# Slots from 256 on: from each expert's step to one place at the layer's end

## The chip, the cores and the metric

The kernel runs on one core of a Trainium2 chip. The metric is the device time of one execution in microseconds (us). Three runs of the kernel before gave 1459.17, 1465.08 and 1466.83; their median, 1465.08, is the time to which the prediction refers. One more execution was profiled and took 1460.41 us.

A core has five engines, each with an instruction stream of its own: PE (matrix products), ACT (ScalarE), DVE (VectorE), POOL (GpSimd) and SP (SyncE). In this kernel SP issues nearly all plain DMAs, and POOL issues the gathers and scatters through index lists (software DMA). The engines meet at semaphores.

## The reference

A decoder trunk of two layers over 512 tokens of width 1024, in float32. Each layer is a mixer (layer 0: dilated attention beside an mLSTM; layer 1: sparse attention) and a mixture of experts, each followed by a layer norm with a scaled residual. The change touches the experts alone:

```python
def hier_moe(x, wr_g, br_g, wr_e, br_e, w_gate, w_up, w_down):
    ...
    _, g_idx = lax.top_k(g_logits, 1)                 # one of 4 groups
    ...
    top_v, top_i = lax.top_k(e_logits, MOE_TOP_K)     # 2 of its 4 experts
    e_w = jax.nn.softmax(top_v, axis=-1) * g_w[:, None]
    ...
    h = jax.nn.silu(xc @ wg) * (xc @ wu)              # 16 experts, hidden 512
    h = h * gate of the expert                        # zero where not chosen
    return h @ wd
```

So each token is worked on by 2 of 16 experts. There are 512 x 2 = 1024 pairs of a token and an expert in a layer, 64 for an expert on average, and no bound on how many fall to one but the 512 tokens.

## The kernel before

**Slots and rounds.** A token row of 1024 is kept as two half rows of 512, so a tile of 128 partitions holds 64 tokens. The pairs of an expert are numbered as slots. A round is 64 slots. `route` (in `Moe`) counts the slots of each expert and leaves words with one bit per expert: `flags[0]` says more than 128 slots, `many[.., 1]` more than 64, `many[.., 2]` more than 192, `flags[3]` more than 256.

**The step.** `step(e)` (L1334) is laid out once per expert. On PE: the transposition of expert e's hidden values (`turn_hidden`), its second product for round 0 (`down`, L1190, 16 matmuls), the first product of the next expert, n = e + 1, for round 0 (`up`, L1162, 32 matmuls), then `beyond(e)`, then for each of n and e an If on more than 64 slots: a second round, or one matmul with zeros (`none`, L1168). ACT copies the result of round 0 to y0 (L1375), DVE that of round 1 to y1 (L1373). ACT and DVE together make the gated activation of n in between (`gated`, L1173 and L1174). POOL adds y0 and y1 into the layer's sum in DRAM (hacc) by scatter DMAs (`scatter`, L1122), and fetches the tokens of expert e + 4 (`fetch_rounds`, L1116). Since hacc is read and written by each scatter, y0 of a step waits until y1 of the step before has landed; y0 and y1 of one step hold other tokens and need not wait for each other. y0 and y1 have one buffer each, so ACT's next copy to y0 waits until y0's scatter has landed.

**Beyond 128 slots.** `beyond(e)` (L1193) is one If on `flags[0]` (L1223), the body of which does two rounds on the tile `more`: products, gated activation, two copies (L1218 on ACT, L1216 on DVE) and two scatters. The tokens have been fetched there by `fetch_beyond(e)`, an If of its own on POOL (the If itself is laid out at L1135, as all that go through `if_more`). Inside the body, a second If on `flags[3]` (L1226) does slots 256 to 511 in two more passes of two rounds, each with a gather of its own. All of this uses the weights of expert e while they are still in their buffers; `reload` then gives the buffers to later weights.

**Order.** `InOrder` keeps the order in which the program lays out instructions, on each of PE, ACT, DVE and POOL, and each of these passes each If whose body holds work for it. An engine that skips a body takes its way around, and a wait there holds all behind it. Weights come as 48 chunks of 2 MB a layer in a ring of nine, loaded by SP (L73 and, in four pieces, L77). SP issues in order.

**The end of a layer.** After the last step `run` (L1252) takes a tile for the norm's factors and loads them (`second_gb`, L1623, into `gb`), loads the sum back from hacc (`load_back`, L1437) and does the residual and the norm (`tail`): PE adds the last expert's result (`back`, L1462), DVE adds the two (`add`, L1469), then come the norm's statistics and products (L142 to L178). In layer 0 the last step also holds work on the next mixer's weights (`lows`, L101).

Of the kernel before, what the change touches and what calls it, by code (L numbers as in the profile page):

```python
# [8 lines left out]
F32 = mybir.dt.float32  # L9
# [6 lines left out]
ORDERED = (mybir.EngineType.PE, mybir.EngineType.Activation, mybir.EngineType.DVE)  # L16
# [3 lines left out]
S, D, P = 512, 1024, 128  # L20
NB = S // P
KT = D // P
E, H = 16, 512
# [191 lines left out]
def bank(k, name):  # L215
    return k.ps.tile([P, 512], F32, name=name, bufs={"acc": 2, "s": 2, "pt": 2, "x": 1, "o": 1}[name])
# [51 lines left out]
def run(steps):  # L268
    for f in steps:
        f()  # L270
# [223 lines left out]
def mixer_ab(k, a, moe, prefetch):  # L494
# [99 lines left out]
    bv = slot("c", (P, NB, 4, 129))  # L594
    nc.gpsimd.memset(bv[:, :, :, 128:129], 1.0)
    run(tokens_blocks(k, ch[3], XH, XL, lambda tb, ps: nc.scalar.copy(
        bv[:, tb, :, 0:128], ps.rearrange("p (h e) -> p h e", h=4))))
    loadnext(6)
# [12 lines left out]
    def ev_o(tb, ps):  # L611
        nc.scalar.activation(og[:, tb], ps, AF.Tanh, scale=0.5)
        nc.vector.scalar_tensor_tensor(og[:, tb], og[:, tb], 1.0, hgb, op0=OP.add, op1=OP.mult)

    run(tokens_blocks(k, ch[4], XH, XL, ev_o))
    loadnext(7)

# [332 lines left out]
class Moe:  # L950
# [234 lines left out]
    def down(self, py, h, r, chunk):  # L1185

        for q in range(4):
            c, b = divmod(q, 2)
            for w in range(2):
                self.k.nc.tensor.matmul(py[w * 64:w * 64 + 64], h[:, r, b, c * 64:c * 64 + 64],  # L1190
                                        chunk[q][:, w * 512:w * 512 + 512], start=q == 0, stop=q == 3)

    def beyond(self, e):  # L1193

        k, nc = self.k, self.k.nc
        w = [k.stream.raw[c] for c in k.ch_moe[self.layer][3 * e:3 * e + 3]]
        x = self.more
        s = x[:, 0].rearrange("p (r a) -> p r a", r=2)
        idx, wt = self.got[e]

        def rounds():
            t = self.xt.tile([P, 2, 4, P], F32, name="xm", bufs=1)
            self.turn(x, t)
            ps = [bank(k, "s") for _ in range(2)]
            self.up(ps[0], t, 0, w)
            self.if_more(ORDERED[0], 2, e, lambda: self.up(ps[1], t, 1, w), lambda: self.none(ps[1]))
            for r in range(2):
                self.gated(s[:, r], ps[r], wt[:, 2 + r, 1:2])
            h = t[:, 0].rearrange("p (r a) b -> p r a b", r=2)
            self.turn_hidden(s, h)  # L1210
            py = [bank(k, "s") for _ in range(2)]
            self.down(py[0], h, 0, w[2])
            self.if_more(ORDERED[0], 2, e, lambda: self.down(py[1], h, 1, w[2]), lambda: self.none(py[1]))
            for r in range(2):
                if r:
                    nc.vector.tensor_copy(x[:, r], py[r])  # L1216
                else:
                    nc.scalar.copy(x[:, r], py[r])  # L1218
            for r in range(2):
                self.scatter(x[:, r], idx[:, 2 + r:3 + r])  # L1220

        over = nc.snap(self.flags[0] & (1 << e))
        with k.tc.If(over > 0, label=f"over{self.layer}_{e}"):  # L1223
            rounds()
            many = nc.snap(self.flags[3] & (1 << e))
            with k.tc.If(many > 0):  # L1226
                for j in range(2, 4):
                    self.one_hot(e, self.oho, j * P)
                    pp = bank(k, "pt")[:, 0:12]
                    self.collect(e, self.oho, pp, 6)  # L1230
                    self.slots(e, 2, pp, 6)
                    for r in range(2):
                        self.fetch(x[:, r], idx[:, 2 + r:3 + r])
                    rounds()

    def load(self, m, queue=None):

# [14 lines left out]
    def run(self, following, finish):  # L1252


        k, nc, st = self.k, self.k.nc, self.k.stream
        pe, act, dve, pool = ORDERED + (mybir.EngineType.Pool,)
        self.rows = [k.moe.tile([P, 2, 512], F32, name=f"rows{i}", bufs=1) for i in range(4)]
        self.more = self.rows[3]
        self.ox = k.moe.tile([P, 2, P], F32, name="hs", bufs=2)
        self.oho = k.early.tile([P, NB, 2 * P], BF16, name="oho", bufs=1)  # L1260
        self.zeros = k.small.tile([P, 512], BF16, name="zeros")
        self.iota = k.small.tile([P, 2 * P], BF16, name="iota")
        self.xt = k.early
        self.got = {}
        self.oh, self.x, self.s = {}, {}, {}

        self.load(RING - 1)
        with k.order:
            nc.gpsimd.memset(self.zeros, 0.0)
            nc.vector.tensor_copy(self.iota.rearrange("p (r i s) -> p r i s", r=2, i=2),  # L1270
                                  k.iota.rearrange("p (r s) -> p r s", r=2)[:, :, None].to_broadcast([P, 2, 2, 64]))
            later, weights = self.route()
            for e in range(2):
                self.got[e] = self.place()
                self.hot(e, False)
                pp = bank(k, "ox"[e])[:, 0:2]
                self.collect(e, self.oh[e], pp, 1)
                self.slots(e, 0, pp, 1)
                self.fetch_rounds(e)
            nc.gpsimd.memset(self.oho, 0.0)  # L1280
            self.load(RING - 2, nc.gpsimd)
            ex = later()
            self.turned(0)
            weights(ex)
            for e in range(2):
                self.beyond_hot(e)
                self.find(e)
        self.order = InOrder(k, ORDERED + (pool,))
        with self.order:
            for e in range(-1, E):  # L1290
                self.step(e, following)
        gb, emit = finish()
        self.load_back(2, NB, after=k.gb_load)
        with self.order:
            self.tail(self.t, self.accs, gb, emit)
# [502 lines left out]
```

## Time and profile before

| | |
|---|---|
| runs, median (lowest, highest) | 1465.08 us (1459.17, 1466.83) |
| profiled execution | 1460.41 us, of which the span of instructions is 1458.5 us |
| busy: PE, DVE, ACT, POOL | 1268.8, 560.1, 410.1, 288.2 us |
| read from and written to DRAM | 287.29 MB and 35.69 MB |
| weights and other plain loads (queue q1) | 257.97 MB |
| software DMA (queue q0) | 39.42 MB |

The experts of layer 0 take the span from about 340 to 700 us, those of layer 1 from about 1060 to 1430 us. A busy engine is not an engine at its peak. The rows further down give a start in us from the span's start, a length in us, the engine, the line of the kernel, the operation with its tiles, how many instructions were merged into the row (x16), and in brackets how long the engine stood idle before it and what it waited for. "<-issue" means that nothing in the profile shows a reason. A "q" behind an engine's name is its sequencer, which does branches and waits.

### The profile page before, as it was taken

The page shows a single profiled execution, that of the slowest core. Times are in us where ns is not written, and L with a number is a line of the kernel's source. Part 1 is how long each engine was busy: PE and PEld are TensorE (multiplying, and loading weights), DVE is VectorE, ACT ScalarE, POOL GpSimd, SP SyncE. Part 2 cuts the span into 40 slices and gives each one's busy share as a digit, 9 for nine tenths or more (in the row PEclk, how much of TensorE's full clock was granted, in tenths as well). Part 3 has the DMA queues.
Part 4 walks back from the last instruction along what each step waited for, and adds up shares of the span by engine and source line. Part 5 has one row for each costly group of instructions (what it writes and reads, how often), then busy time and mean ns, then how long its engine had stood idle before and what let it go on. Part 6 is the DMA issues. An engine that isn't in the chain of part 4 may idle for free. (4 is left out here: it accounts for less than half of the span.)

```text
span 1458.5 us, 18462 instructions
## 1 busy us (share of the span) xinstructions
PE 1268.8 (87%) x6379; PEld 732.6 (50%) x6404; DVE 560.1 (38%) x1452; ACT 410.1 (28%) x852; POOL 288.2 (20%) x319
## 2 busy tenths in 40 slices
PE   7999999986889988898599999999779875877985
PEld 6777864573333333333277877777633322333332
DVE  4845644474211101211466546877631111221114
ACT  4333434441111000111235445655410010111112
POOL 2200000033222111322320000000422113222222
PEclk9999999986999999999899999999779998999998
DMA  8721250192797427899644530303725447999953
GB/s 296 247 94 58 93 210 22 68 365 81 306 351 289 185 61 278 281 390 337 240 163 151 224 123 15 146 22 143 298 99 191 178 141 251 376 395 384 370 151 145
DMA packets 64136, 299.80 MB, mean 206 GB/s; under 512 B 15426, under 2 KB 15586, under 8 KB 36560
## 3 DMA queue, kind: packets, MB, share of 16 engines
q1 hardware_dynamic: 42624, 257.97, 45.8%
q0 software_dynamic: 21328, 39.42, 9.8%
q8 instruction: 111, 1.82, 0.5%
q14 instruction: 73, 0.60, 0.1%
HBM read 287.29 MB, written 35.69 MB: 221 GB/s over the span
## 5 line engine op out<-in xcount | busy, mean ns | idle before, releaser
L1162 PE MATMUL acc<-raw,xt 128*64 128x512 f32 x1376 | 307.4, 600 | 7.0 <-PEq L1223 4.3
L1174 DVE SCALAR_TENSOR_TENSOR hs<-hs,wsl,acc 128x256 f32<-128x256 f32 x64 | 30.6, 480 | 471.2 <-ACT hs L1173 236.1
L1162 PEld LDWEIGHTS acc<-raw,xt 128*64 128x64 f32 x1376 | 102.7, 139 | 205.4 <-issue 185.7
L1122 POOL DMA_INDIRECT hacc<-y,idx x60 | 95.7, 1596 | 316.7 <-issue 138.6
L1190 PE MATMUL s<-raw,hm 128*64 128x512 f32 x464 | 119.1, 660 | 21.7 <-ACT hm L1183 13.1
L101 DVE TENSOR_TENSOR sl<-raw,sh 128x1024 fp32r<-128x1024 f32 x80 | 96.3, 1224 | 51.0 <-ACT sh L93 50.0
L1375 ACT COPY y<-s 128x512 f32<-128x512 f32 x30 | 17.6, 586 | 301.9 <-DMA hacc<-y,idx 278.0
L1116 POOL DMA_INDIRECT rows<-hmid,idx x72 | 75.7, 1052 | 102.2 <-issue 88.8
L93 ACT CAST sh<-raw 128x1024 fp32r<-128x1024 f32 x80 | 81.8, 1048 | 32.0 <-PE acc L119 10.7
L1190 PEld LDWEIGHTS s<-raw,hm 128*64 128x64 f32 x464 | 35.6, 151 | 86.0 <-issue 59.6
L1173 ACT ACTIVATE hs<-acc 128x256 f32<-128x256 f32 x64 | 24.6, 385 | 178.2 <-PE acc L1162 160.6
L1190 PE MATMUL s<-sh,hm 128*64 128x512 f32 x224 | 51.1, 598 | 8.3 <-ACT hm L1183 4.2
L1168 PE MATMUL s<-zeros 128*128 128x512 bf16 x23 | 10.1, 438 | 54.3 <-DVEq L1223 33.8
L1151 PE MATMUL pt<-ident,rows 128*128 128x128 f32 x288 | 45.8, 309 | 12.2 <-issue 6.4
L396 ACT ACTIVATE p<-p,smx 128x512 f32<-128x512 f32 (+1 forms) x96 | 54.0, 563 | 6.0 <-DVE smx L394 5.4
L394 DVE CUSTOM_DVE_ANT_0 p<-s,bt 128x384 f32<-128x384 f32 (+3 forms) x69 | 34.6, 503 | 49.5 <-PE s L877 34.5
L1151 PEld LDWEIGHTS pt<-ident,rows 128*128 128x128 f32 x288 | 38.1, 158 | 27.9 <-issue 25.0
L1162 PE MATMUL s<-raw,xm 128*64 128x512 f32 x160 | 42.7, 655 | 10.4 <-ACT xm L1155 9.6
L287 PE MATMUL acc<-sh,h 128*128 128x512 f32 x112 | 46.7, 417 | 0.2
L1168 PEld LDWEIGHTS <-zeros 128*128 128x128 bf16 x48 | 4.6, 96 | 83.5 <-issue 78.3
L477 POOL DMA_DIRECT2D bt<-rows x16 | 8.8, 552 | 190.2 <-DVE smx L394 188.3
L118 PE MATMUL acc<-h,sh 128*128 128x512 f32 x112 | 45.2, 403 | 0.0
(440 smaller groups left out, 2375.0 us busy)
## 6 DMA issues: line engine op xcount, KB each, us to landing
raw<-moe SPq DMA_DIRECT2D x168, 1024.0 KB
sh<-moe SPq DMA_DIRECT2D x40, 512.0 KB
raw<-cw SPq DMA_DIRECT2D x18, 1024.0 KB
raw<-abw SPq DMA_DIRECT2D x12, 1024.0 KB
rows<-row POOLq DMA_DIRECT2D x8, 640.0 KB
bt<-rows POOLq DMA_DIRECT2D x16, 256.0 KB
raw<-abo SPq DMA_DIRECT2D x4, 1024.0 KB
hmid<-s SPq DMA_DIRECT2D x8, 512.0 KB
```

Source lines behind the costliest of these rows:

```text
L93: k.nc.scalar.copy(h, r)
L101: (engine or self.k.nc.vector).tensor_tensor(lo, r, h.bitcast(F32), op=OP.subtract)
L118: nc.tensor.matmul(out, lh, rh, start=start, stop=False)
L287: nc.tensor.matmul(ps, yh[q][:, c], h[:, r], start=q == 0, stop=False)
L394: nc.vector.tensor_tensor_reduce(p, sp, bias, scale=1.0, scalar=3e38, op0=OP.add, op1=OP.min, accum_out=st[:, 0:1])
L396: nc.scalar.activation(p, p, AF.Exp, bias=st[:, 0:1], scale=-1.0, accum_out=st[:, 1:2])
L1116: self.k.nc.gpsimd.indirect_dma_start(out=x, out_offset=None, in_=self.h.rearrange("a (b c) -> (a b) c", b=2), in_offset=bass.IndirectOffs ...
L1122: return self.k.nc.gpsimd.indirect_dma_start(out=self.acc.rearrange("a (b c) -> (a b) c", b=2), out_offset=bass.IndirectOffsetOnAxis(ap=id ...
L1151: nc.tensor.transpose(px[:, b], x[:, r, b * P:b * P + P], self.k.ident)
L1162: self.k.nc.tensor.matmul(ps[c * 64:c * 64 + 64], t[:, r, b, i * 64:i * 64 + 64], w[c][kt // 2][:, kt % 2 * 512:kt % 2 * 512 + 512], start ...
L1174: nc.vector.scalar_tensor_tensor(s, s, weight, ps[:, 256:512], op0=OP.mult, op1=OP.mult)
L1190: self.k.nc.tensor.matmul(py[w * 64:w * 64 + 64], h[:, r, b, c * 64:c * 64 + 64], chunk[q][:, w * 512:w * 512 + 512], start=q == 0, stop=q ...
```

## The change

The inner If goes out of `beyond`, so that a step does at most slots 128 to 255 beside its first two rounds. A new function `deep` comes behind the last step of a layer: one If on `flags[3]` being other than zero, that is, on whether any expert of the layer has more than 256 slots. Its body goes over all 16 experts, loads the three weight chunks of each again through POOL's queue into the pool `moer`, and does the two passes of two rounds with them, as the inner block did; slots that an expert doesn't have are read and written out of bounds and so dropped. At its end it reads blocks 0 and 1 of the sum back from hacc again, which the last step had already done. The two rounds themselves are now the method `two_rounds`, unchanged but for who decides on the second round.

```diff
@@ -1190,48 +1190,61 @@
                 self.k.nc.tensor.matmul(py[w * 64:w * 64 + 64], h[:, r, b, c * 64:c * 64 + 64],
                                         chunk[q][:, w * 512:w * 512 + 512], start=q == 0, stop=q == 3)
 
-    def beyond(self, e):
+    def two_rounds(self, e, w, second):
 
         k, nc = self.k, self.k.nc
-        w = [k.stream.raw[c] for c in k.ch_moe[self.layer][3 * e:3 * e + 3]]
         x = self.more
         s = x[:, 0].rearrange("p (r a) -> p r a", r=2)
         idx, wt = self.got[e]
-
-        def rounds():
-            t = self.xt.tile([P, 2, 4, P], F32, name="xm", bufs=1)
-            self.turn(x, t)
-            ps = [bank(k, "s") for _ in range(2)]
-            self.up(ps[0], t, 0, w)
-            self.if_more(ORDERED[0], 2, e, lambda: self.up(ps[1], t, 1, w), lambda: self.none(ps[1]))
-            for r in range(2):
-                self.gated(s[:, r], ps[r], wt[:, 2 + r, 1:2])
-            h = t[:, 0].rearrange("p (r a) b -> p r a b", r=2)
-            self.turn_hidden(s, h)
-            py = [bank(k, "s") for _ in range(2)]
-            self.down(py[0], h, 0, w[2])
-            self.if_more(ORDERED[0], 2, e, lambda: self.down(py[1], h, 1, w[2]), lambda: self.none(py[1]))
-            for r in range(2):
-                if r:
-                    nc.vector.tensor_copy(x[:, r], py[r])
-                else:
-                    nc.scalar.copy(x[:, r], py[r])
-            for r in range(2):
-                self.scatter(x[:, r], idx[:, 2 + r:3 + r])
-
+        t = self.xt.tile([P, 2, 4, P], F32, name="xm", bufs=1)
+        self.turn(x, t)
+        ps = [bank(k, "s") for _ in range(2)]
+        self.up(ps[0], t, 0, w)
+        second(lambda: self.up(ps[1], t, 1, w), lambda: self.none(ps[1]))
+        for r in range(2):
+            self.gated(s[:, r], ps[r], wt[:, 2 + r, 1:2])
+        h = t[:, 0].rearrange("p (r a) b -> p r a b", r=2)
+        self.turn_hidden(s, h)
+        py = [bank(k, "s") for _ in range(2)]
+        self.down(py[0], h, 0, w[2])
+        second(lambda: self.down(py[1], h, 1, w[2]), lambda: self.none(py[1]))
+        for r in range(2):
+            if r:
+                nc.vector.tensor_copy(x[:, r], py[r])
+            else:
+                nc.scalar.copy(x[:, r], py[r])
+        for r in range(2):
+            self.scatter(x[:, r], idx[:, 2 + r:3 + r])
+
+    def beyond(self, e):
+
+        k, nc = self.k, self.k.nc
+        w = [k.stream.raw[c] for c in k.ch_moe[self.layer][3 * e:3 * e + 3]]
         over = nc.snap(self.flags[0] & (1 << e))
         with k.tc.If(over > 0, label=f"over{self.layer}_{e}"):
-            rounds()
-            many = nc.snap(self.flags[3] & (1 << e))
-            with k.tc.If(many > 0):
+            self.two_rounds(e, w, lambda many, few: self.if_more(ORDERED[0], 2, e, many, few))
+
+    def deep(self):
+
+        k, nc = self.k, self.k.nc
+        with k.tc.If(self.flags[3] > 0, label=f"deep{self.layer}"):
+            for e in range(E):
+                w = []
+                for c in k.ch_moe[self.layer][3 * e:3 * e + 3]:
+                    t = k.moer.tile([P, 4096], F32, name="raw")
+                    nc.gpsimd.dma_start(t, k.stream.chunks[c])
+                    w.append([t[:, q * 1024:(q + 1) * 1024] for q in range(4)])
                 for j in range(2, 4):
+                    self.got[e] = self.place()
                     self.one_hot(e, self.oho, j * P)
                     pp = bank(k, "pt")[:, 0:12]
                     self.collect(e, self.oho, pp, 6)
                     self.slots(e, 2, pp, 6)
                     for r in range(2):
-                        self.fetch(x[:, r], idx[:, 2 + r:3 + r])
-                    rounds()
+                        self.fetch(self.more[:, r], self.got[e][0][:, 2 + r:3 + r])
+                    self.two_rounds(e, w, lambda many, few: many())
+            for tb in range(2):
+                nc.gpsimd.dma_start(self.accs[:, tb], self.acc[tb * P:(tb + 1) * P, :])
 
     def load(self, m, queue=None):
 
@@ -1289,6 +1302,7 @@
         with self.order:
             for e in range(-1, E):
                 self.step(e, following)
+            self.deep()
         gb, emit = finish()
         self.load_back(2, NB, after=k.gb_load)
         with self.order:
```

Lines behind the change are 14 higher in the kernel after (L1371 is L1385, L1462 L1476, L1469 L1483, L1623 L1637). The three places below are in the order of the instructions as the two kernels were built; "waits" names semaphores, DMASW0 to 7 the eight lanes on which software DMAs report in turn.

POOL before, from the end of the inner body through the ways around the inner If (L1226) and the outer (L1223) and around the next expert's `fetch_beyond` (L1135), to the step's own scatters and fetches (rows_2477 is the tile `more`, y_2972 y0, y_2973 y1):

```order
L1122 DMA hacc_59<-rows_2477,idx 1024x512 [waits DMASW7_49,DVE_49]
L1226 UNCONDITIONAL_BRANCH
L1226 ISA [waits DMASW4_49,DMASW5_49,DMASW3_49,DMASW6_49,DMASW2_49,DMASW7_49,DMASW1_49,DMASW0_49]
L1226 UNCONDITIONAL_BRANCH
L1223 ISA [waits DMASW4_49,DMASW5_49,DMASW3_49,DMASW6_49,DMASW2_49,DMASW7_49,DMASW1_49,DMASW0_49]
L1223 UNCONDITIONAL_BRANCH
...
L1135 ISA [waits DMASW2_49,DMASW1_49]
L1135 UNCONDITIONAL_BRANCH
L1122 DMA hacc_59<-y_2972,idx 1024x512 [waits DMAHW0_49,DMAHW6_49,DMASW3_49,DMAHW7_49,DMASW0_49,Activation_49]
```

POOL after, from one step's scatter of y1 and its two fetches through the whole of the next step's `beyond`:

```order
L1122 DMA hacc_59<-y_2973,idx 1024x512 [waits DMASW4_49,DVE_49]
L1116 DMA rows_2475<-hmid_57,idx 128x512 [waits DMASW5_49,PE_49]
L1116 DMA rows_2475<-hmid_57,idx 128x512 [waits DMASW6_49,PE_49]
...
L1224 COMPARE_AND_BRANCH
L1135 UNCONDITIONAL_BRANCH x2
L1122 DMA hacc_59<-rows_2477,idx 1024x512 [waits DMASW4_49,DMASW7_49,Activation_49,Pool_49]
L1122 DMA hacc_59<-rows_2477,idx 1024x512 [waits DMASW7_49,DVE_49]
L1224 UNCONDITIONAL_BRANCH
L1224 ISA [waits DMASW7_49,DMASW0_49]
```

The inner If with its way around is gone, the body ends in a branch without a wait, and the way around the outer If names two lanes and not eight; the eight lanes now stand once a layer, at L1230.

DVE before, at the end of layer 0's experts: the last difference for the residual, the two products for the next mixer's weights, and the residual's first block:

```order
L1371 TENSOR_TENSOR raw<-s,raw 128x512 [waits Activation_49]
L101 TENSOR_TENSOR sl<-raw,sh 128x1024 [waits DMAHW0_49]
L101 TENSOR_TENSOR sl<-raw,sh 128x1024
L1469 TENSOR_TENSOR raw<-raw,s 128x512 [waits DMAHW5_49,DMAHW4_49,DMAHW6_49,DMAHW1_49,PE_49]
L1469 TENSOR_TENSOR raw<-raw,s 128x512 [waits PE_49]
```

DVE after, at the same place, the body of `deep` left out:

```order
L1385 TENSOR_TENSOR raw<-s,raw 128x512 [waits Activation_49]
L101 TENSOR_TENSOR sl<-raw,sh 128x1024 [waits DMAHW0_49]
L101 TENSOR_TENSOR sl<-raw,sh 128x1024
L1230 COMPARE_AND_BRANCH
...
L1230 UNCONDITIONAL_BRANCH
L1230 UNCONDITIONAL_BRANCH [waits DVE_49]
L1483 TENSOR_TENSOR raw<-raw,s 128x512 [waits DMAHW4_49,DMAHW5_49,DMAHW1_49,DMAHW6_49,DMASW3_49,PE_49]
```

The If on `flags[3]` stands between the products and the residual, and PE's first matmul of the residual (L1476) now waits for DVE behind that If.

## Rows read from the trace of the kernel before

**Rows 1.** The page: busy time (share of the span) xinstructions.

```profile
PE 1268.8 (87%) x6379; PEld 732.6 (50%) x6404; DVE 560.1 (38%) x1452; ACT 410.1 (28%) x852; POOL 288.2 (20%) x319
```

**Rows 2.** The waits: who waited for whom, us in total, times, longest.

```profile
ACT y L1375 <- DMA hacc<-y,idx: 278.0, 25, 24.8
...
PE s L1168 <- DVEq L1223: 33.8, 6, 15.9
```

**Rows 3.** The timeline of POOL in a loaded step of layer 1.

```profile
1295.94 1.63 POOL L1122 DMA_INDIRECT hacc<-y,idx  x1 [12.78 <-issue]
1297.87 1.58 POOL L1122 DMA_INDIRECT hacc<-y,idx  x1 [0.30 <-issue]
...
1301.13 1.05 POOL L1116 DMA_INDIRECT rows<-hmid,idx  x1 [0.31 <-issue]
1315.51 1.63 POOL L1122 DMA_INDIRECT hacc<-y,idx  x1 [13.34 <-issue]
```

**Rows 4.** Line 1223 on POOL: times min/median/max in ns, first and last start.

```profile
L1223 POOLq EVENT_SEMAPHORE  x112: 17/43/14041, 362.2 to 1424.0; - x112
```

**Rows 5.** Line 1218, the copy that each pass makes on ACT.

```profile
L1218 ACT COPY rows<-s x4: 586/586/586, 486.4 to 1190.4; 128x512 f32<-128x512 f32 x4
```

**Rows 6.** The timeline of ACT behind those scatters.

```profile
1305.29 0.59 ACT L1375 COPY y<-s 128x512 f32<-128x512 f32 x1 [14.63 <-DMA hacc<-y,idx]
```

**Rows 7.** The timeline of PE in layer 1's experts.

```profile
1173.01 7.86 PE L1162 MATMUL s<-raw,xm 128*64 128x512 f32 x26 [5.30 <-ACT xm L1155]
...
1224.16 0.59 PE L1168 MATMUL s<-zeros 128*128 128x512 bf16 x1 [15.89 <-DVEq L1223]
...
1231.52 7.04 PE L1162 MATMUL acc<-raw,xt 128*64 128x512 f32 x32
...
1246.03 7.04 PE L1162 MATMUL acc<-raw,xt 128*64 128x512 f32 x32
...
1306.97 0.59 PE L1168 MATMUL s<-zeros 128*128 128x512 bf16 x1 [5.75 <-DVEq L1223]
...
1344.30 0.59 PE L1168 MATMUL s<-zeros 128*128 128x512 bf16 x1 [6.04 <-DVEq L1223]
...
1404.00 7.04 PE L1162 MATMUL acc<-raw,xt 128*64 128x512 f32 x32
```

**Rows 8.** The timeline of PE in layer 0's experts.

```profile
515.67 16.62 PE L1162 MATMUL s<-raw,xm 128*64 128x512 f32 x64 [3.75 <-ACT xm L1155]
...
579.02 5.32 PE L1190 MATMUL s<-raw,hm 128*64 128x512 f32 x16 [5.33 <-DVEq L1223]
```

**Rows 9.** Line 1226 on POOL, the increment behind the inner If.

```profile
L1226 POOLq INC_SWDGE_SEM  x4: 1532/1676/1819, 503.9 to 1207.9; - x4
```

**Rows 10.** The timeline of POOL behind that increment's last.

```profile
1213.01 1.57 POOL L1122 DMA_INDIRECT hacc<-y,idx  x1 [9.06 <-DMA rows<-hmid,idx]
```

**Rows 11.** A window: busy by engine, PE clock, DMA share, GB/s.

```profile
1245.00:1375.00 130.00, 107.36 (x575) 45.02 (x579) 22.89 (x60) 17.39 (x35) 39.13 (x31) 0.92 1.00 387
```

**Rows 12.** The timeline of SP, weight loads of layer 1.

```profile
1272.71 40.67 SPq L73 DMA_DIRECT2D raw<-moe  x16
...
1368.19 6.74 SPq L77 DMA_DIRECT2D sh<-moe  x4
1379.28 18.48 SPq L73 DMA_DIRECT2D raw<-moe  x6
```

**Rows 13.** The timelines of SP and of DVE at the end of layer 0.

```profile
708.95 0.33 SPq L1623 DMA_DIRECT2D s<-gb  x1
...
717.60 2.48 DVE L101 TENSOR_TENSOR sl<-raw,sh 128x1024 fp32r<-128x1024 f32 x2
...
722.75 0.75 DVE L155 SCALAR_TENSOR_TENSOR raw<-raw,lnmv,s 128x512 f32<-128x512 f32 x1
```

**Rows 14.** PE's branches at lines 1135 and 1223, ns.

```profile
L1135 PEldq COMPARE_BRANCH  x96: 65/208/3897, 350.2 to 1429.3; - x96
...
L1223 PEldq COMPARE_BRANCH  x32: 77/450/2712, 367.8 to 1422.8; - x32
```

More of the change, by code (lines that the diff above doesn't have):

```diff
@@ L1191, in down @@
                                         chunk[q][:, w * 512:w * 512 + 512], start=q == 0, stop=q == 3)
+    def two_rounds(self, e, w, second):
+        k, nc = self.k, self.k.nc
+        x = self.more
+        s = x[:, 0].rearrange("p (r a) -> p r a", r=2)
+        idx, wt = self.got[e]
+        t = self.xt.tile([P, 2, 4, P], F32, name="xm", bufs=1)
[17 more added lines that the diff above has]
+            self.scatter(x[:, r], idx[:, 2 + r:3 + r])
     def beyond(self, e):
@@ L1196, in beyond @@
         w = [k.stream.raw[c] for c in k.ch_moe[self.layer][3 * e:3 * e + 3]]
-        x = self.more
-        s = x[:, 0].rearrange("p (r a) -> p r a", r=2)
-        idx, wt = self.got[e]
-        def rounds():
-            t = self.xt.tile([P, 2, 4, P], F32, name="xm", bufs=1)
-            self.turn(x, t)
-            ps = [bank(k, "s") for _ in range(2)]
-            self.up(ps[0], t, 0, w)
-            self.if_more(ORDERED[0], 2, e, lambda: self.up(ps[1], t, 1, w), lambda: self.none(ps[1]))
-            for r in range(2):
-                self.gated(s[:, r], ps[r], wt[:, 2 + r, 1:2])
-            h = t[:, 0].rearrange("p (r a) b -> p r a b", r=2)
-            self.turn_hidden(s, h)
-            py = [bank(k, "s") for _ in range(2)]
-            self.down(py[0], h, 0, w[2])
-            self.if_more(ORDERED[0], 2, e, lambda: self.down(py[1], h, 1, w[2]), lambda: self.none(py[1]))
-            for r in range(2):
-                if r:
-                    nc.vector.tensor_copy(x[:, r], py[r])
-                else:
-                    nc.scalar.copy(x[:, r], py[r])
-            for r in range(2):
-                self.scatter(x[:, r], idx[:, 2 + r:3 + r])
         over = nc.snap(self.flags[0] & (1 << e))
         with k.tc.If(over > 0, label=f"over{self.layer}_{e}"):
-            rounds()
-            many = nc.snap(self.flags[3] & (1 << e))
-            with k.tc.If(many > 0):
+            self.two_rounds(e, w, lambda many, few: self.if_more(ORDERED[0], 2, e, many, few))
[8 more added lines that the diff above has]
+                    w.append([t[:, q * 1024:(q + 1) * 1024] for q in range(4)])
                 for j in range(2, 4):
+                    self.got[e] = self.place()
                     self.one_hot(e, self.oho, j * P)
```

## The prediction

> **What bounds the kernel now.** I read the page first: of a span of 1458.5 us the matrix engine (PE) works 87% and the vector engine (DVE) 38% [rows 1]. So time can only be won where PE stands still, and the chain at the foot of the page is no help there, since it covers only the last microseconds. I therefore went to the view of waits. The reader is to see two rows in it: ScalarE (ACT) waits 278.0 us in 25 places, before its copy of y0 at L1375, for an earlier scatter-add into hacc to land, and PE waits 33.8 us in six places at L1168 for DVE to come past the If of L1223 [rows 2]. The second is the first one's shadow: behind the copy of y0, ACT has the activation of the next expert's first round, DVE multiplies its result before it reaches L1223, and PE's matmul at L1168 has to see DVE there. So what times the scatters of y0 is what can stall PE.
>
> The timeline of GpSimd (POOL) in a loaded step shows what times them [rows 3]. y0 and y1 of one expert are issued at 1295.94 and 1297.87, the second fetch at 1301.13, and the next y0 only at 1315.51, with 13.34 us idle that no engine is named for. The order of the kernel before says what POOL does there: the way around the If of L1223 ends in an instruction ("ISA") that waits for all eight lanes of software DMA, since the body it skips uses all eight. The two fetches issued a moment earlier are on such lanes. In the profile that is the event wait of L1223 on POOL, 14.041 us at the most [rows 4], and behind it stands an increment, priced below.
>
> **The change part by part.** It takes the rounds for slots from 256 on out of the step's If and puts them under one If per layer. The inner body itself costs and saves nothing, since it isn't run: the copy at L1218, one for each pass, has four executions, two a layer [rows 5], as many as the Ifs that were taken, and each run of the inner block would add two. So the edit acts through what stands around a body that is skipped, three things.
>
> First, the step without slots over 128 (28 of 32). The body now has two DMAs, so POOL waits on its way around it for two lanes, those of the two scatters that it skips, whose last users landed long before; the fetches drop out. y0 must still wait for y1 of the step before, which adds into the same rows. From y0's issue at 1295.94 to ACT's copy that waits for it, at 1305.29, are 9.35 us [rows 3, 6]; with the same for y1, it lands at 1297.87 + 9.35 = 1307.2 (an estimate). POOL's two increments pass meanwhile. So y0 could go at about 1307.7 and not at 1315.51: 7.8 us earlier, and ACT's next copy with it. What PE gains is only its stall. Layer 1 has two long ones of this kind, 5.75 and 6.04 us; the one of 15.89 stands behind a step with more slots (below) [rows 7]. The other three of the six in rows 2 hold 33.8 - 27.7 = 6.1 us together; of these I take 2. Upper end in layer 1: 11.8 us for the long ones; lower end: nothing.
>
> Second, the four steps with more slots. There, POOL waited at the inner If (L1226) for all lanes, the second scatter of the body among them, then spent 1.53 to 1.82 us on the increment, and about as much again at the next If (L1135, an estimate from the first). The last of these increments starts at 1207.9, when everything has landed [rows 9]; y0 follows at 1213.01 [rows 10]. Now nothing stands at the end of the taken body, the other increment passes while the scatter is on its way, and y0 goes with the landing, 0.7 us for POOL's own instructions (an estimate: two DMAs in a row stand 0.3 us apart [rows 3]): 1213.01 - 1207.9 - 0.7 = 4.4 us earlier. PE stood 5.30 (waiting for xm) and 15.89 us behind the two of layer 1 [rows 7], 3.75 and 5.33 behind those of layer 0 [rows 8]. So 4.4 + 4.4 = 8.8 us in layer 1, 3.75 + 4.4 = 8.2 in layer 0. Lower end 0, if something else is late at once.
>
> How much of layer 1's two parts reaches its end is set by the weights. From 1245 to 1375 the DMA engines are busy at a share of 1.00 [rows 11]. SP issues 40 pieces, two turns of the ring of nine chunks or six experts, from 1272.71 to 1368.19 + 6.74 = 1374.93: 17.0 us an expert [rows 12]. PE takes (1404.00 - 1231.52) / 10 = 17.25 us an expert over ten of them, where an undisturbed one takes 1246.03 - 1231.52 = 14.5 [rows 7]. The first part is safe: the loads of the full stretch are released by PE's steps ahead of it, so 8.8 us earlier there is 8.8 us earlier throughout. Of the 11.8 us, some is slack that the weights have: the queue stands idle from 1374.93 to 1379.28, 4.35 us, because PE hasn't yet freed a buffer [rows 12], so by then the weights are ahead of PE. Between 0 and 11.8 I take 10, since no stall of PE's in this stretch names a weight. Layer 1: -18.8. Layer 0, whose weights are not at their limit in its steps: -8.2. The three short stalls, in either layer: -2.
>
> Third, the new If behind the last step, which every engine passes. Its ISA on POOL still names eight lanes, but hacc must have landed by then anyway. In layer 0 DVE reaches it only behind the two products for the next mixer's weights (L101), 717.60 + 2.48 = 720.08 [rows 13], and PE's first matmul for the residual, which before ran beside them, now waits for DVE to be past. So the addition at L1469 no longer begins when the products end: I take 2.1 us, no more than their own 2.48. SP's load of gb is issued at 708.95 and used at 722.75 [rows 13]. If SP is let past the new If only behind DVE, it leaves at 720.3; with 9.35 us to land, as y0, it is there at 729.65 and not at 722.75 + 2.1: another 4.8, or nothing if SP needn't wait. In layer 1 no product stands there and gb is wanted late: 1 (an estimate for one more wait on DVE). I take +3 and +1, from 0 to 12 in all.
>
> Reading code is the fourth cost. PE's branches at L1135 take 0.208 us in the middle and 3.897 at the most; those at L1223, which jump over three rounds of code, 0.450 and 2.712 [rows 14]. The jump over the new body is far longer, and the step's is shorter. By these rows the new If costs PE at most 3.9 us a layer, and 32 shorter jumps save at most 32 x (0.450 - 0.077) = 12 us; in many of them PE has to wait anyway, so I take 0 net.
>
> The Trainium skill, "Runtime: NRT & Kernel Launch", section "Instruction fetch mechanics", says that a taken branch out of the window already loaded stops the engine until a DMA has brought the target page, which speaks against this change. The maxima of the rows would fit such fetches, the medians would not. By the rule, with one fetch of 3.897 us for PE in each layer, the sum would be 7.8 us worse; by the median it stays.
>
> The sum: -18.8 - 8.2 - 2 + 4 = -25. The profiled execution took 1460.41, so 1435.4 in its terms; the runs' median is 1465.08, 4.67 above, which I add: 1440 us.
>
> **The rivals.**
> A is the forecast: the lanes set the time, and PE gets most of its stalls back.
>
> B: the gain is hidden. The DMA share of 1.00 speaks for it: a weight queue that is full gains nothing from an earlier scatter, and scatters that go earlier fall among the weights. Against it speaks SP's idle 4.35 us. Then only the starts are left, -8.8 in layer 1 and half of layer 0's -8.2, with the tails +4: -9, or 1456.
>
> C, slower: the new If becomes a barrier of which the ends pay the whole. In each layer the jump costs PE 3.9 and then DVE 3.9, one behind the other, layer 0 has the 2.1 us of products and 4.8 for gb on top: 15.6 + 6.9 = +22.5. It decides once the steps give less than that, as under B, where they give 13: +9.5, 1474.6. For it: on all engines the skipped body is the longest of the program. Against: in both layers DVE's own jump can run while PE is still at the last matmuls, and PE's jumps over the three rounds take 0.450 us in the middle [rows 14].
>
> D: the change doesn't do what it says, the deep body runs. It would load every expert's weights again, at 17.0 us an expert 272 us a layer. The count of four at L1218 is against it.
>
> E: the step's shorter jumps also bring code sooner. The rows' bound is 12 us; with 8 of it, 1432. For it speaks the median of 0.450 at L1223 where L1135 has 0.208 [rows 14]; against it, that none of PE's long stalls names its own sequencer [rows 7, 8]. The skill's rule on branches would be the reason for it.
>
> **How the numbers follow.** A 0.62, B 0.18, E 0.12, C 0.07, D 0.01. A's own range is 1426 to 1452: the tails' ends (-4, +8), the 11.8 us (-2, +10), the short stalls (-4, +2) and layer 0 (-1, +8), not all at once. For eight in ten I need B's side but not all of C: 1420 to 1459. A measurement of this kernel can tell 0.5% from no change, 7.3 us: below 1457.8 is faster, above 1472.4 slower. Faster: A, E and half of B, 0.62 + 0.12 + 0.09 = 0.83. Within: the other half of B and a third of C, 0.11. Slower: the rest of C, and D, 0.06.
>
> **What would show it.** Right: on POOL no event wait of more than 3 us on the way around the step's If; y0 issued about 10 us behind the y1 before it, and 5 to 8 earlier after the second fetch; ACT's 278 us much less; PE's six stalls at L1168 gone or under 2 us; in layer 1 the ten experts from L1162's expert 5 on in 16 us each, the whole stretch started some 9 us earlier; in both tails the addition for block 0 behind the new If by 1 to 3 us. Wrong: stalls of PE that name the weights' DMAs in place of DVE (B); branches of 2 us or more at the new If on both PE and DVE and the time from the last expert's matmuls to the first addition up by 5 or more (C); y0's scatter still waiting for the fetches, which would end the argument altogether.

## The result, and the profile after

The kernel after takes 1411.28 us (median of three runs, 1410.49 to 1414.25) against 1465.08: a ratio of 0.9647, 95% interval 0.9599 to 0.9695. It is faster by 53.8 us; the forecast was 25 us faster, and the lower end of its range was 1420. The profiled execution took 1410.49 us.

What the forecast looked for on POOL and ACT is there. The view of POOL's waits at the If of the step (L1224 now) and the view of waits, kernel after:

```profile
L1224 POOLq EVENT_SEMAPHORE  x28: 17/17/17, 361.5 to 1368.1; - x28
```
```profile
ACT y L1389 <- PE s L1190: 88.5, 22, 6.4
ACT y L1389 <- DMA hacc<-y,idx: 65.6, 8, 12.7
```

POOL no longer waits on its way around (14.041 us at the most before [rows 4]), and ACT waits 65.6 us in 8 places for a scatter to land, where it was 278.0 in 25 [rows 2]. Of PE's stalls at L1168 the longest left are 2.66 us for DVE and 2.93 us for its own sequencer.

To see where 50 us of the span went, I laid PE's rows of L1162 (an expert's first product) of both kernels side by side. Each entry is the time that PE has gained on the kernel before between two such rows, the first from the span's start and the last to its end; up(n) is the row of expert n's first round:

| stretch | gained, us | forecast |
|---|---|---|
| layer 0, up to the expert at 453.70 after (460.63 before) | 6.9 | 0 |
| layer 0, over its two steps with more than 128 slots, to 567.23 (590.01) | 15.8 | 8.2 |
| rest of layer 0's experts | 3.5 | 2, with layer 1's |
| from there to layer 1's up(2) at 1090.74 (1116.76) | -0.2 | -3 |
| layer 1, over its two such steps, up(2) to up(5) | 23.4 | 8.8 |
| layer 1, up(5) to up(15) | 3.2 | 10 |
| the end | -2.5 | -1 |

Two of these rows, kernel before and kernel after:

```profile
590.01 7.04 PE L1162 MATMUL acc<-raw,xt 128*64 128x512 f32 x32
...
1116.76 7.04 PE L1162 MATMUL acc<-raw,xt 128*64 128x512 f32 x32
```
```profile
567.23 7.04 PE L1162 MATMUL acc<-raw,xt 128*64 128x512 f32 x32
...
1090.74 7.04 PE L1162 MATMUL acc<-raw,xt 128*64 128x512 f32 x32
```

The loaded stretch of layer 1 gave less than forecast: PE takes (1351.41 - 1182.12) / 10 = 16.9 us an expert there, hardly less than the 17.25 of before, and one stall of PE now names a weight. PE's timeline, kernel after:

```profile
1182.12 7.04 PE L1162 MATMUL acc<-raw,xt 128*64 128x512 f32 x32
...
1293.74 8.78 PE L1162 MATMUL acc<-raw,xt 128*64 128x512 f32 x30 [3.89 <-DMA raw<-moe]
...
1351.41 7.04 PE L1162 MATMUL acc<-raw,xt 128*64 128x512 f32 x32
```

By up(10) PE had gained 11.9 us there (73.6 us from up(5), 85.5 before), and by up(15) it had lost 8.7 of them again.

Most of the excess is in the four steps with more than 128 slots: 39.2 us for a forecast of 17. Here is the second such step of layer 0 in the kernel before, on ACT (the body's copy), SP and POOL:

```profile
541.91 0.59 ACT L1218 COPY rows<-s 128x512 f32<-128x512 f32 x1 [7.29 <-PE s L1190]
```
```profile
542.00 5.46 SPq L73 DMA_DIRECT2D raw<-moe  x4
```
```profile
543.27 1.63 POOL L1122 DMA_INDIRECT hacc<-rows,idx  x1 [27.49 <-ACTq L1226]
554.08 1.59 POOL L1122 DMA_INDIRECT hacc<-rows,idx  x1 [9.18 <-DVE y L1373]
567.53 1.57 POOL L1122 DMA_INDIRECT hacc<-y,idx  x1 [11.86 <-issue]
```

and the same in the kernel after:

```profile
527.43 0.59 ACT L1215 COPY rows<-s 128x512 f32<-128x512 f32 x1 [8.99 <-PE s L1190]
```
```profile
516.09 5.26 SPq L73 DMA_DIRECT2D raw<-moe  x4
```
```profile
528.78 1.63 POOL L1122 DMA_INDIRECT hacc<-rows,idx  x1 [33.59 <-ACT rows L1215]
534.51 1.59 POOL L1122 DMA_INDIRECT hacc<-rows,idx  x1 [4.09 <-DMA hacc<-rows,idx]
538.97 1.57 POOL L1122 DMA_INDIRECT hacc<-y,idx  x1 [2.88 <-ACT xt L1155]
```

The reader is to look at SP first. The next weights leave 0.1 us behind the body's copy before, and 11.3 us ahead of it after. The program text has not moved them. But the inner block, though skipped, was the last reader of the expert's three chunks, so their buffers came free only behind the body; now the two chunks of the first product come free after it. Issued together with the body's scatters, the loads go through the DMA engines beside them: from the first scatter to the second, which waits for it, are 10.8 us before and 5.7 after, and the DMA engines are busy in between at a share of 1.00 before and 0.36 after. y0 goes 25.6 us behind the copy before and 11.5 after: 14.1 us, where the forecast had 4.4. In the other three such steps it goes 12.1, 13.5 and 9.6 us earlier behind the copy.

A part of layer 0's 15.8 us is not idle time. Over that stretch PE is busy 112.6 us before, at a mean granted clock of 0.95, and 107.9 us after, at 0.98: 4.8 us. Behind the stall of 3.75 us, 64 products take 16.62 us before [rows 8]; from 515.7 to 519.0 the granted clock is 0.50, the lower of the two levels (1.2 GHz). The same 64 products in the kernel after, without the stall, run at 1.00 (2.4 GHz). The window of PE before (its length, PE's busy time, the granted clock, the DMA engines' share, GB/s) and the row after:

```profile
515.70:519.00 3.30, 3.30 (x8) 0.50 0.20 62
```
```profile
502.11 14.01 PE L1162 MATMUL s<-raw,xm 128*64 128x512 f32 x64 [0.28 <-ACT xm L1155]
```

So a stall that goes takes the slow clock behind it along.

### The profile page after: what moved, and what is told of

Its sections match the earlier page's. It is cut to its first block, busy times and chain, and to the rows that moved or that the text cites. A ratio compares the mean times of both kernels' runs of the same rounds, so it can differ in the third digit from the quotient of the medians.

```text
span 1408.4 us, 18333 instructions
## 1 busy us (share of the span) xinstructions
PE 1260.5 (89%) x6404; PEld 726.7 (52%) x6404; DVE 561.1 (40%) x1452; ACT 410.9 (29%) x852; POOL 288.2 (20%) x319
## 5 line engine op out<-in xcount | busy, mean ns | idle before, releaser
L1162 PE MATMUL acc<-raw,xt 128*64 128x512 f32 x1376 | 312.6, 603 | 9.1 <-DMA raw<-moe 3.9
L1162 PEld LDWEIGHTS acc<-raw,xt 128*64 128x64 f32 x1376 | 106.2, 139 | 206.9 <-issue 188.3
L1190 PE MATMUL s<-raw,hm 128*64 128x512 f32 x464 | 111.7, 620 | 15.1 <-ACT hm L1183 13.6
L1190 PEld LDWEIGHTS s<-raw,hm 128*64 128x64 f32 x464 | 34.3, 142 | 73.7 <-issue 54.1
L1190 PE MATMUL s<-sh,hm 128*64 128x512 f32 x224 | 52.0, 598 | 4.4 <-ACT hm L1183 4.3
L1151 PE MATMUL pt<-ident,rows 128*128 128x128 f32 x288 | 40.8, 288 | 8.3 <-issue 8.3
L1151 PEld LDWEIGHTS pt<-ident,rows 128*128 128x128 f32 x288 | 34.5, 147 | 22.7 <-issue 20.8
L410 PE MATMUL pt<-ident,p 128*128 128x128 f32 x240 | 44.4, 284 | 0.8 <-DVE smx L397 0.8
L120 PE MATMUL acc<-h,sl 128*128 128x512 f32 x112 | 44.5, 397 | 0.5 <-DVE sl L101 0.5
L118 PE MATMUL acc<-raw,sh 128*128 128x512 f32 x112 | 44.5, 397 | 0.0
```

What stands on the lines that cost most here:

```text
L118: nc.tensor.matmul(out, lh, rh, start=start, stop=False)
L120: nc.tensor.matmul(out, ll, rh, start=False, stop=stop)
L410: nc.tensor.transpose(pp[:, P * (i - kb):P * (i - kb) + P], Pt[:, POFF[i] + P * kb:POFF[i] + P * kb + P], k.ident)
L1151: nc.tensor.transpose(px[:, b], x[:, r, b * P:b * P + P], self.k.ident)
L1162: self.k.nc.tensor.matmul(ps[c * 64:c * 64 + 64], t[:, r, b, i * 64:i * 64 + 64], w[c][kt // 2][:, kt % 2 * 512:kt % 2 * 512 + 512], start ...
```

## The experiments

Four of them add to the kernel after a block that isn't run, inside the step's If. e1 adds the whole inner block again, with `deep` kept:

```diff
             self.two_rounds(e, w, ...)
+            many = nc.snap(self.flags[3] & (1 << e))
+            with k.tc.If(many > 0):
+                x, idx = self.more, self.got[e][0]
+                for j in range(2, 4):
+                    self.one_hot(e, self.oho, j * P)
+                    pp = bank(k, "pt")[:, 0:12]
+                    self.collect(e, self.oho, pp, 6)
+                    self.slots(e, 2, pp, 6)
+                    for r in range(2):
+                        self.fetch(x[:, r], idx[:, 2 + r:3 + r])
+                    self.two_rounds(e, w, ...)
```

e2 has only the DMAs in the loop:

```diff
+                    for r in range(2):
+                        self.fetch(x[:, r], idx[:, 2 + r:3 + r])
+                    for r in range(2):
+                        self.scatter(x[:, r], idx[:, 2 + r:3 + r])
```

e3 is e1 without the fetches and without the scatters at the end of `two_rounds`; e4 is e3 with another operand in place of the weights:

```diff
-                    self.two_rounds(e, w, ...)
+                    z = x.rearrange("p a b -> p (a b)")
+                    self.two_rounds(e, [[z] * 4] * 3, ...)
```

> The kernel after, with the inner block for slots from 256 on put back into each step (it is not run), and the If at the layer's end kept. Three theories of where the 54 us came from. LANES: POOL's way around the If waits for all eight software-DMA lanes. HOLD: the inner block is the last reader of the expert's weights, so in a step with over 128 slots all three chunks come free only at the end of the body, later, and their loads fall on the body's scatters. CODE: PE's jumps over the longer body wait for code. All three expect the whole gain gone here: 1465, plus the 2 to 5 us that the If at the end costs: 1466 to 1470. Below 1455, part of the gain would lie in none of them.

> As e1, but the inner block holds only its DMAs (four fetches and four scatters, so again all eight lanes), no products: no weight is read there and PE has almost nothing to jump over. It leaves the work on slots from 256 on out of the block; it is not run. LANES expects nearly the whole loss: 1445 to 1460. HOLD and CODE expect the time of the kernel after, 1411 to 1417. On POOL, LANES expects the long event waits at the outer If back, up to about 14 us.

> As e1, but the inner block holds only the index work and the products with the expert's weights, no DMA: POOL's way around waits for two lanes, the weights are held to the end of the body, and PE's code is as long as before. It leaves the fetches and scatters of slots from 256 on out; the block is not run. LANES expects 1411 to 1416. HOLD expects a loss in the four steps with over 128 slots, by 4 to 6 us each: 1425 to 1438. CODE alone expects 8 to 12 us, at PE's zeros products in layer 0: 1419 to 1424.

> As e3, but the products of the inner block read the token tile in place of the weights (not run): code as long as in e3, and no weight is held. It leaves out the DMAs of slots from 256 on and has wrong operands there. LANES: 1411 to 1416. HOLD: the same 1411 to 1416, and the difference to e3 is its price. CODE: 1419 to 1424, the same as e3.

Measured, as median and ratio to the kernel before (its median 1462.05 here): e1 1469.03, 1.0053 (1.0023 to 1.0083); e2 1433.65, 0.9813 (0.9777 to 0.9849); e3 1434.10, 0.9817 (0.9784 to 0.9850); e4 1424.37, 0.9750 (0.9707 to 0.9794).

e1: the whole gain is gone, and 0.5% more, which fits the price of the If at the end (below). e2: the lanes cost 22 us, not the 34 to 49 that LANES alone expected. e3 and e4: 23 and 13 us where LANES expected none, so all three causes are there: e4 is the price of code, and e3 less e4, 10 us, that of holding the weights (the two intervals overlap a little; e5 below is a second measure). PE's timeline in e4 shows the code at two steps of layer 0:

```profile
389.39 0.58 PE L1168 MATMUL s<-zeros 128*128 128x512 bf16 x1 [5.13 <-remote]
...
406.96 0.59 PE L1168 MATMUL s<-zeros 128*128 128x512 bf16 x1 [3.19 <-issue]
```

The kernel before has them too:

```profile
391.28 0.58 PE L1168 MATMUL s<-zeros 128*128 128x512 bf16 x1 [4.95 <-remote]
...
408.87 0.58 PE L1168 MATMUL s<-zeros 128*128 128x512 bf16 x1 [3.20 <-issue]
```

In the kernel after, the same two rows come 1.27 and 1.48 us behind the end of the products before them:

```profile
388.90 0.38 PE L1168 MATMUL s<-zeros 128*128 128x512 bf16 x1
...
403.32 0.38 PE L1168 MATMUL s<-zeros 128*128 128x512 bf16 x1 [0.36 <-DVEq L1224]
```

Over the two steps (up(2) to up(4) of layer 0) PE takes 36.9 us before, 39.8 in e4 and 28.6 in the kernel after, so they hold 8.2 us of the change's gain and 11.1 of e4's 13. The first gap is one branch of PE at L1135 in the kernel before (it takes 4.063 us in e4). In the kernel after that branch takes 0.2 us, and the long one is that of the step's own If, beside products that end at 387.6. Kernel before, then kernel after:

```profile
L1135 PEldq COMPARE_BRANCH  x1: 3897/3897/3897, 386.7 to 386.7; - x1
```
```profile
L1224 PEldq COMPARE_BRANCH  x1: 3839/3839/3839, 383.4 to 383.4; - x1
```

So in the kernel with the long body PE comes past the step's own If and then stands at the next branch. That it waits there for its code is inferred, from what e4 adds and from a queue that the profile calls "instruction", in packets, MB and share, kernel before and kernel after:

```profile
q8 instruction: 111, 1.82, 0.5%
```
```profile
q8 instruction: 92, 1.51, 0.4%
```

It has 116 packets in e4 and 92 in e2.

What e1 to e4 leave open is the sum: 22 + 10 + 13 = 45, but e1 lost 58. e5 holds the weights with twenty-four matmuls in the loop, with less code than e4 (106 packets in that queue); e6 has the fetches of e2 ahead of these and its scatters behind them:

```diff
+                    ps = bank(k, "s")
+                    for c in w:
+                        for q in range(4):
+                            nc.tensor.matmul(ps[0:64], x[:, 0, 0:64], c[q][:, 0:512], start=q == 0, stop=q == 3)
```

> The kernel after with an inner If in each step's body (not run) that holds only twenty-four matmuls, which read the expert's three weight chunks, and no DMA: the weights are held to the body's end as before, PE's code is hardly longer, POOL waits for two lanes. HOLD as read from e3 less e4: all of the loss in one step of layer 1, none in layer 0, because each step has some slack before y0's scatter: 1418 to 1424. If the loss in e3 was code: 1409 to 1414.

> As e5 with the eight DMAs of e2 beside it (not run): HOLD and LANES together, with hardly any code. SLACK, that the two delays add up in front of y0's scatter and are paid only beyond one slack common to both: 22 (e2) + 10 (e5) + 12 for layer 0's two steps over 128 slots, in which neither costs anything alone = 1411 + 44 = 1455, 1449 to 1460, and y0's scatter in those steps about 12 us later than in the kernel after. ADD, that the two prices simply add up: 1411 + 32 = 1443, 1438 to 1447.

e5 took 1427.93 us, 0.9769 (0.9744 to 0.9794), 4 us above what HOLD gave: 17 us over the kernel after, not 10. e6 took 1460.14, 0.9981 (0.9960 to 1.0002), at the upper end of SLACK's range and far above ADD's. With e5's own 17, ADD would give 1411 + 22 + 17 = 1450, so 10 us remain that the two have only together. Then e10, which is e1 with the other operand of e4 in its `two_rounds`: all the code and all the DMAs, no weights held.

> The kernel before's inner block put back with all its DMAs and all its code, but its products read the token tile in place of the weights (not run; it has wrong operands there): LANES and CODE without HOLD. With the loads released early, y0's scatter in the four steps over 128 slots should be 4 to 6 us later than in the kernel after, not 11 to 14, and the two steps of layer 0 should cost nothing again: 1411 + 22 (e2) + 13 (e4) = 1446, 1438 to 1452. If the weights' release were no cause, 1465 to 1470 as e1.

1443.18 us, 0.9868 (0.9823 to 0.9913), in the range expected, though layer 0's two steps cost 3.2 us and not nothing (table below): holding the weights is worth 26 us between e10 and e1.

The step shown above, in all of them, from their timelines (us). SP's loads, the second scatter and y0 are counted from the body's copy on ACT; PE is its time from the row of L1162 beside that copy (527.10 in the kernel after) to the third such row behind it (567.23). The last two columns are the two stretches of the table of gains, over both such steps of a layer:

| | weights leave | second scatter | y0 leaves | PE | layer 0's two | layer 1's two |
|---|---|---|---|---|---|---|
| after | -11.3 | 7.1 | 11.5 | 40.1 | 113.5 | 91.4 |
| e2, lanes | -9.7 | 7.1 | 15.7 | 40.1 | 113.1 | 101.7 |
| e10, lanes and code | -9.7 | 7.0 | 15.6 | 40.1 | 116.7 | 101.6 |
| e5, hold | 0.1 | 12.0 | 20.9 | 40.0 | 115.7 | 108.9 |
| e6, lanes and hold | 0.1 | 12.1 | 25.7 | 48.5 | 127.8 | 115.0 |
| before, all | 0.1 | 12.2 | 25.6 | 47.3 | 129.4 | 114.8 |

The rows of POOL behind it, e2, e5 and e6:

```profile
531.40 1.58 POOL L1122 DMA_INDIRECT hacc<-rows,idx  x1 [4.11 <-DMA hacc<-rows,idx]
540.04 1.57 POOL L1122 DMA_INDIRECT hacc<-y,idx  x1 [7.06 <-issue]
```
```profile
542.39 1.58 POOL L1122 DMA_INDIRECT hacc<-rows,idx  x1 [9.05 <-DMA hacc<-rows,idx]
551.26 1.57 POOL L1122 DMA_INDIRECT hacc<-y,idx  x1 [7.28 <-DMA hacc<-rows,idx]
```
```profile
543.68 1.59 POOL L1122 DMA_INDIRECT hacc<-rows,idx  x1 [9.08 <-DVE y L1399]
557.29 1.57 POOL L1122 DMA_INDIRECT hacc<-y,idx  x1 [12.02 <-issue]
```

The lanes delay y0 by 4.2 us and the held weights by 9.4; together by 14.1. PE doesn't feel either alone, and feels 8.4 us of both: y0 may leave some 21 us behind the copy for nothing, and 25.7 is too late. So neither cause has a price of its own in this step. Over layer 1's two steps it is the other way: 10.3 us for the lanes alone, 17.5 for the held weights alone, and 23.6 for both, less than the sum.

The rest are about the If at the layer's end. e7 leaves out the call of `deep`. e8 and e9 add a hint in the last step that its branch will be taken, e8 for PE alone, e9 for three engines; e11 is the kernel after once more:

```diff
             self.beyond(e)
+            if final:
+                k.tc.mark_branch_hint_location(f"deep{self.layer}", "LikelyTaken", [pe, act, dve])
```

> The kernel after without the If at the layer's end; slots from 256 on, which this input doesn't have, are left out. TAIL, that the If costs what the first addition of each tail is late by (about 2.3 us in either layer): 1405 to 1409. REGAINED, that layer 0 has it back in the next mixer: 1408 to 1410, layer 1's 2.5 alone.

> The kernel after with one instruction more in the last step of a layer: a hint to PE, ahead of the step's last products, that the branch over the deep body will be taken, as each step has one for its own If. If reading code is what PE's branch of 3.34 and 3.85 us does: the branch under 1 us and 1407 to 1410. If the branch waits for something else, or the hint comes too late: 1410 to 1413, and the branch as long as before.

> The kernel after with the hint of e8 for PE, ACT and DVE. In the kernel after, DVE's branch over the deep body in layer 1 is at 1379.5 and its next instruction at 1382.5, ACT's at 1378.8 and 1381.7, while PE's branch lies beside its last products. JUMP: what the tail pays is the time in which DVE (and ACT) get past the jump, and the hint on them saves it: DVE past in under 1 us, from the last difference to the first addition in layer 1 under 4 us in place of 5.65, 1404 to 1409. NOHELP: the hint changes nothing on these engines: 3 us there as before, 1409 to 1413.

> The kernel after once more, unchanged, beside e9 on the same chip, so that differences of less than 1% can be read: 1408 to 1415 by every theory.

e7: 1404.97 us, 0.9604 (0.9576 to 0.9631). e8: 1411.58, 0.9664 (0.9640 to 0.9689). e9: 1414.14, 0.9672 (0.9638 to 0.9706). e11: 1411.61, 0.9653 (0.9616 to 0.9690). So the If costs about 6 us by the medians, though the intervals of e7 and e11 overlap a little, and the hints make no difference that can be told; in e8 PE's branch still takes 2.84 and 3.37 us. In layer 1 the tail shows the price: the last difference and the first addition on DVE, kernel after and e7:

```profile
1379.45 0.69 DVE L1385 TENSOR_TENSOR raw<-s,raw 128x512 fp32r<-128x512 f32 x1 [4.51 <-ACT raw L1384]
1385.10 1.28 DVE L1483 TENSOR_TENSOR raw<-raw,s 128x512 f32<-128x512 f32 x2 [4.96 <-PE s L1476]
```
```profile
1374.05 0.69 DVE L1384 TENSOR_TENSOR raw<-s,raw 128x512 fp32r<-128x512 f32 x1 [4.51 <-ACT raw L1383]
1375.80 1.29 DVE L1482 TENSOR_TENSOR raw<-raw,s 128x512 f32<-128x512 f32 x2 [1.06 <-PE s L1475]
```

5.65 us against 1.75. In between stands DVE's jump. Line 1230 in the kernel after, the branch and the first instruction behind it:

```profile
L1230 PEldq COMPARE_BRANCH  x2: 3340/3596/3852, 689.8 to 1375.5; - x2
...
L1230 DVEq COMPARE_BRANCH  x2: 56/56/56, 690.8 to 1379.5; - x2
...
L1230 DVEq EVENT_SEMAPHORE  x2: 21/21/21, 693.8 to 1382.5; - x2
```

DVE's branch itself reads 0.056 us, but its next instruction comes 3.0 us later, and PE's matmuls wait for it. In layer 1 PE's own 3.340 us lie beside its last products. In e9 DVE's gap is still 3.1 and 3.2 us.

In layer 0 the tail is 2.25 us longer (from the last difference to the addition 5.26 us, 3.01 before). The place is not settled there: DVE's two products end at 693.77, DVE's next instruction behind the jump is at 693.8, and PE's own branch of 3.852 us, behind its last products, ends at 693.7. Kernel after, DVE and PE:

```profile
691.42 2.35 DVE L101 TENSOR_TENSOR sl<-raw,sh 128x1024 fp32r<-128x1024 f32 x2
696.08 1.28 DVE L1483 TENSOR_TENSOR raw<-raw,s 128x512 f32<-128x512 f32 x2 [2.31 <-PE s L1476]
```
```profile
694.00 2.17 PE L1476 MATMUL s<-raw 64*128 64x512 f32 x8 [3.84 <-DVEq L1230]
```

e12 moves the If ahead of the last copy and difference (and takes the call at the layer's end away):

```diff
-            py = bank(k, "s")
+            py = bank(k, "acc" if final else "s")
             self.if_more(pe, 1, e, lambda: self.down(py, h, 1, down), lambda: self.none(py))
+            if final:
+                self.deep()
             keep(1, py)
```

> The kernel after with the If for slots from 256 on moved forward a little: between the last step's second product and the copy and difference (ACT, DVE) of its result, which takes another PSUM bank for that. All engines then jump over the deep body while PE is at that product. BESIDE: the tail's price goes, as in e7, since ACT and DVE are past the jump before the product ends: from the last difference to the first addition in layer 1 under 2.5 us in place of 5.65, 1403 to 1408. STILL: the engines reach the jump no earlier, because each waits at the If before it, or the code that is fetched next is late instead: 1409 to 1414.

```profile
1377.85 0.58 ACT L1383 CAST raw<-acc 128x512 fp32r<-128x512 f32 x1 [3.39 <-PE acc L1190]
```
```profile
1380.48 0.69 DVE L1384 TENSOR_TENSOR raw<-acc,raw 128x512 fp32r<-128x512 f32 x1 [5.29 <-issue]
1382.06 1.29 DVE L1484 TENSOR_TENSOR raw<-raw,s 128x512 f32<-128x512 f32 x2 [0.88 <-PE s L1477]
```

From the last difference to the addition are 1.58 us, as in BESIDE, but the time, 1409.73 us and 0.9642 (0.9616 to 0.9669), can't be told from the kernel after's and lies in STILL's range. The difference itself is late now: it starts 2.05 us behind the end of ACT's copy, with no reason shown. Counted from the end of PE's last products at L1190, the addition in layer 1 comes 6.31 us later in the kernel after, 4.25 in e12 and 2.41 in e7, and in layer 0 7.96, 7.37 and 5.70. So e12 saves 2.7 of the 6.2 us that e7 saves in the two tails; the rest of the price has moved ahead of the difference.

## Why the prediction was wrong in size

The direction and the mechanism on POOL were right: the way around the inner and outer If waits for lanes, and e2 gives that 22 us, where the forecast's terms of this kind were 29 without the tails. The prediction left out what the inner block holds, and what its code costs, and it took a stall to be worth its own length.

**Second part, the steps with more slots (8.8 and 8.2 us; 23.4 and 15.8 measured).** The step that failed is "y0 goes with the landing ... 4.4 us earlier". As the lanes' share it was right: e2 has 4.2 in the step shown. But it took the landing of the second scatter as it was. I had followed the removed block on POOL alone, as a user of lanes; it is also a reader of the weights, on PE, and SP waits for the last reader. That the loads leave 11 us earlier, and the scatters land sooner for it, was in none of the rivals; y0 went 9.6 to 14.1 us earlier in the four steps. I had given it a lower end of 0, an upper one of 1 us more in layer 0 and none in layer 1. That PE's stalls of 5.30 and 15.89 us [rows 7] might go altogether, 21.2 us, would have been one; layer 1 gained 23.4. e10 against e1 is the measure of the weights, 26 us in the presence of the other two. In layer 0 I had 8.2 of the stalls' 9.1 us; what was missing there is the clock, 4.8 us, against "What PE gains is only its stall", and PE's ways past the inner If, 1.00 and 0.87 us.

**Fourth part, reading code (0 taken, 12 the bound).** e4 measures 13 us. Rival E had the cause and the size (8 us, with 12 as the bound), against it stood that no long stall of PE names its own sequencer. But the rows that carry it, 4.95 and 3.20 us in layer 0, are put down to "remote" and "issue", and I had looked at stalls by the name of the engine waited for. Nor is it spread over 32 shorter jumps at the step's If, as the bound of 12 had it: PE's branches there got longer (1.094 us in the middle at L1224, 0.450 before [rows 14]), beside products. The cost lay at the next branch, in two steps.

The Trainium skill, "Runtime: NRT & Kernel Launch", section "Instruction fetch mechanics", has it that a taken branch to a place outside the loaded window waits until a DMA has fetched it. That spoke for the change in the steps, as rival E said, and against it at the layer's end. The runs fit both, the second as a gap of 3.0 us behind DVE's branch; that a fetch fills these gaps is not shown.

**First part, the loaded stretch (10 us; 3.2 measured).** Here the rows fit rival B: with the long stalls at L1168 gone, PE gains 11.9 us and gives 8.7 back, waits for weights once by name (3.89 us), the DMA engines are busy at a share of 1.00 from 1182.1 to 1351.4, and an expert takes 16.9 us against the 17.0 in which SP issued its loads [rows 12]. That SP stood idle for 4.35 us once was no slack of the whole stretch. That the first parts' gains pass through it whole was right.

**The tails (4 us; about 6 by e7).** The total is near. Layer 1's term, 1 us, was mis-sized: 3.9 us, for DVE's jump, which the sum had at nothing. Layer 0's, 3 us, measured 2.25, and whether DVE's two products or one of the jumps set it can't be told there. gb was not late: it leaves at 681.64, ahead of the If, and is used at 698.84. Whether layer 0's loss reaches further is open: from its last expert's first product to layer 1's first are 373.64 us before, 373.52 after, and 371.06 in e7.

**Rivals C and D** did not come: the count at L1215 is four again, and C's barrier came to some 6 us, not 22.5.

## What to carry to other kernels

A skipped block still acts through what the program must assume of it: it is the last user of lanes, and the last reader of buffers. So when a block is moved, list for each tile it reads who waits to overwrite it, and for each engine what the way around it waits for. Two delays in front of one wait share its slack: in a step of layer 0, 4.2 and 9.4 us cost nothing each and 8.4 together, and in layer 1's steps 10.3 and 17.5 alone made 23.6, so prices measured one at a time do not add, in either direction. And a stall is worth more than its length when PE's clock is low behind it.

## What had not been expected of the hardware

At the end of layer 1, a branch of 0.056 us on DVE was followed by 3.0 us until its next instruction, while PE's branch at the same If is itself 3.340 us long: the length of a branch row is not a jump's price on every engine. A scatter of a body took 10.8 us until the next could go when four weight loads left with it, and 5.7 when they had left 11 us before. Behind a stall of 3.75 us PE's granted clock was 0.50, and the 64 products that followed took 16.62 us in place of 14.01.
